# Order edges around the matrix-memory heads: query halves behind the score weighting, mask load first, conditioning row behind the target rows

## The chip, the cores and the metric

The kernel runs on one core of a Trainium2 chip. The metric is the device time of one execution, in microseconds (us); before the change it is 1218.85 us, the median of three runs (1218.58 to 1222.32). One core has five engines with a queue each, and each queue is worked off in order: TensorE (PE in the profile) multiplies matrices into eight accumulation banks, VectorE (DVE) and ScalarE (ACT) work element by element, GpSimd (POOL) does the same more slowly and here mostly issues transfers, and SyncE (SP) issues the other transfers.

## The reference, cut to what matters

One layer of a diffusion backbone works on 512 latent tokens and 256 context tokens of width 1024. The part that the change touches is the matrix-memory branch, which has four heads of 256 channels. For every head and each of two directions it computes decay-weighted scores and applies them to the values:

```python
s = jnp.einsum("bhtd,bhsd->bhts", qb, kb) * jnp.exp(logD - m_t[..., None])
num = jnp.einsum("bhts,bhsd->bhtd", s, vb) + ...
den = jnp.sum(s, axis=-1) + ...
hb = num / jnp.maximum(jnp.abs(den), jnp.exp(-m_t))[..., None]
```

The reference scans in chunks of 64 tokens. The kernel uses the equal form without the scan: for a target token t and a source token s, latent or context, the score q·k is multiplied by the exponential of (a row that depends on the target) + (a column that depends on the source), with a mask inside the diagonal block.

A second part is the conditioning: the vector c goes through silu and a matrix of 6 x 1024 columns, and the results shift, scale and gate the stream (`modT` in the kernel).

## The kernel before, in words

Every product keeps fp32 accuracy with three passes: each operand x is split into a high half (ScalarE copies it to a rounded 32-bit format, line 214) and a low half (VectorE subtracts the high half from x, line 215), and TensorE computes high·high, high·low and low·high into the same bank (lines 233 to 235). Nearly all TensorE time goes into these three lines, and a weight or an operand can be used only when both halves are there.

Loads that are to be split go through a ring of four staging buffers named `wr` (line 239 for weights, line 903 for the heads' operands; the conditioning weights `in_wada` use it too, line 357). A buffer of the ring is free when VectorE has made the low half, or has done the multiplication for the conditioning.

The kernel is written in program order, and a planner then sets the order of each engine's queue from estimated times; it may place later work ahead of earlier work if its estimate says that it is ready sooner. It also adds all waits. Two means are used to steer it: `behind()` (line 578) and `tc.issue_after(x)`. What is traced inside such a block, and runs on the engine of instruction x, is queued behind x on that engine. This fixes the order of issue; it is no wait for x to finish, and it has no effect on instructions of other engines.

The stage around the change (about 556 to 710 us) works like this:

- `load_head(h)` (line 910) loads queries (`wr<-qd`) and two key tiles (`wr<-kd`) of a head and splits them into `uh`/`ul` and the two `K` buffers. Queries have two buffers, so the next head's can be loaded while one is in use. Keys have one buffer for each half.
- `load_values(h)` (line 922) loads and splits the values into `vh`/`vl`, one buffer each.
- `target_rows()` (line 848) is done once: TensorE transposes 14 small tiles, and ScalarE copies them in four pieces into `rrow` (line 855).
- `decay(h, d)` (line 872) broadcasts a row with a matmul against the selector `sel` (line 880), adds the mask with another (line 882), and ScalarE takes exponentials of the banks into `dx` and `dy` (line 886).
- `weigh(h, ...)` (line 931) computes q·k for six source tiles s. Each takes six matmuls of 512 columns into a bank of the pool `psH`, which has four banks. VectorE multiplies the bank by 1/64 and by the decay tile (line 943), once for each direction; then the bank is free.
- `halves` (line 945) splits the weighted scores, and `values(h, d, ...)` (line 951) multiplies them with the values into the four banks of `psG` and divides by the denominator (lines 962 to 968).

The loop over heads (line 1354) does, for h = 0, 1, 2: `load_head(h+1)`, first `decay` of head h+1, `values(h, 0)`, second `decay`, one tile of the other branch's projection (`ph_tiles`, line 1299, for h = 1 and 2), `weigh(h+1)`, `values(h, 1)`, `load_values(h+1)`, `halves`, another projection tile, and `head_norm`. `ph_tiles` first reloads its 16 operand tiles from memory (`hTh<-hhd`, `hTl<-hhd`, lines 226 and 227), issued by GpSimd. Output gates are computed as fillers before that (`gate_tile`, line 702): ScalarE applies a tanh (line 708) and GpSimd stores the result (line 709).

`ada_row()` (line 378) makes the conditioning row `crow`: one load (line 380), one tanh on ScalarE (line 381) and two multiplications on VectorE (lines 382 and 383). `steps` and `beside` then advance the conditioning products (line 372).

Of the kernel before, what the change touches and what calls it, by code (L numbers as in the profile page):

```python
# [8 lines left out]
F32 = mybir.dt.float32  # L9
F32R = mybir.dt.float32r  # L10
AF = mybir.ActivationFunctionType
ALU = mybir.AluOpType
# [147 lines left out]
def build(nc, tc, I, out, dbg=None):  # L160
# [14 lines left out]
    act, dve, pe, gp = nc.scalar, nc.vector, nc.tensor, nc.gpsimd  # L175
    dma = nc.sync.dma_start
# [8 lines left out]
    def T(p, shape, dt=F32, tag=None, bufs=None):  # L185
        uid[0] += 1
        p = HOME.get(tag, p)
        bufs = BUFS.get(tag, bufs)
        kw = {} if bufs is None else {"bufs": bufs}
        nm = f"{tag or 't'}_{uid[0]}"  # L190
        return p.tile(list(shape), dt, tag=tag or nm, name=nm, **kw)
# [9 lines left out]
    def bank(p=None):  # L201
        return T(p or psH, [128, 512], F32, "bank")
# [5 lines left out]
    def load(p, key, shape, tag=None, src=None):  # L208
        t = T(p, shape, F32, tag or key)
        dma(t[:], I[key] if src is None else src)  # L210
        return t
# [51 lines left out]
    for key, shp in VECS:  # L263
        m = int(np.prod(shp))
# [113 lines left out]
    def ada_row():  # L378
        th = T(PW, [128, WMAX], F32, "wr")[:, :D]
        dma(crow[:], I["crow"].broadcast_to([128, D]))  # L380
        act.activation(th, crow[:], AF.Tanh, scale=0.5)
        dve.tensor_scalar_mul(crow[:], crow[:], 0.5)
        dve.scalar_tensor_tensor(crow[:], th, 1.0, crow[:], op0=ALU.add, op1=ALU.mult)
# [329 lines left out]
    def gate_math(p):  # L713
# [38 lines left out]
        ps = bank()  # L752
        L = ps[:, 0:48].rearrange("p (b d h) -> p b d h", b=6, d=2)
        fc = S([2, 6, 4], "fc")
# [93 lines left out]
    def target_rows():  # L848
        rr = T(PM_, [128, 512], F32R, "rrow")
        gp.memset(rr[:].bitcast(F32), 0.0)  # L850
        for q, (g0, n) in enumerate(((0, 4), (4, 4), (8, 3), (11, 3))):
            pr = bank()
            for j in range(n):
                pe.transpose(pr[:16, 128 * j : 128 * j + 128], G["rhl"][:, g0 + j].bitcast(F32), ident)
            act.activation(rr[32 * q : 32 * q + 16, : 128 * n], pr[:16, : 128 * n], AF.Copy)
        G["rr"] = rr

# [43 lines left out]
    def staged(src, n, hi, lo, a=None):  # L903
        t = T(PW, [128, WMAX], F32, "wr")[:, :n]
        if a:
            t = t.rearrange("p (a b) -> p a b", a=a)
        dma(t, src)
        split(hi, lo, t)

    def load_head(h):  # L910

        kh, kl = (T(PT, [128, 2048], F32R, "K")[:, :1536].rearrange("p (a b) -> p a b", a=2) for _ in range(2))
        qh, ql = T(PT, [128, 2, SEQ], F32R, "uh"), T(PT, [128, 2, SEQ], F32R, "ul")

        staged(qd[:, 2 * h : 2 * h + 2], 2 * SEQ, qh[:], ql[:], 2)
        if h == 0:
            fill(next(cf))
        for i in range(2):
            staged(kd[:, 2 * h + i], SEQ + CTX, kh[:, i], kl[:, i])
        return (qh, ql), (kh, kl)  # L920

    def load_values(h):
        Vh, Vl = T(PM_, [128, 6, NV], F32R, "vh"), T(PM_, [128, 6, NV], F32R, "vl")
        gp.memset(Vh[:, :, 256:257].bitcast(F32), 1.0)
        gp.memset(Vh[:, :, 257:258].bitcast(F32), 0.0)
        gp.memset(Vl[:, :, 256:258].bitcast(F32), 0.0)
        for b, n in ((0, 4), (4, 2)):
            staged(vd[:, h, b : b + n], 256 * n, Vh[:, b : b + n, :256], Vl[:, b : b + n, :256], n)
        return Vh, Vl

    def weigh(h, qq, kk, Dm):

        (qh, ql), (kh, kl) = qq, kk
        for s in (4, 5, 0, 1, 2, 3):
            ps = bank()
            tk = slice(128 * s, 128 * s + 128)
            for i in range(2):
                mm3(ps[:], kh[:, i, tk], kl[:, i, tk], qh[:, i], ql[:, i], i == 0, i == 1)
            for d in range(2):
                t0, n = PIECE[d][s][:2]  # L940
                dst = piece(Dm[d], d, s)
                sv = ps[:, 128 * t0 : 128 * (t0 + n)].rearrange("p (a b) -> p a b", a=n)
                dve.scalar_tensor_tensor(dst, sv, 1.0 / 64, dst, op0=ALU.mult, op1=ALU.mult)

    def halves(Dm):
        wh, wl = parts(F32R), parts(F32R)
# [3 lines left out]

    def values(h, d, W, V, den, hs):
        (wh, wl), (Vh, Vl) = W, V
        for t in range(4):
# [255 lines left out]
    def fill(n):  # L1209
        for _ in range(n):  # L1210
            if fills:
                fills.pop(0)()
# [68 lines left out]
    PM_ = PMS.enter_context(pool("pm", reuse_waits="tile"))  # L1281
# [29 lines left out]
    fill(next(cf))  # L1311
    L = load_head(0)
    fill(next(cf))
    V = load_values(0)
    sel = T(PM_, [128, 32], F32R, "sel")
    selr = load(PM_, "sel", [128, 32], "selr")
    act.activation(sel[:], selr[:], AF.Copy)
    mask = T(PM_, [128, 2, 128], F32R, "mask")
    maskr = load(PM_, "mask", [128, 2, 128], "s2")
    act.activation(mask[:], maskr[:], AF.Copy)  # L1320
    identr = T(PM_, [128, 128], F32R, "identr")
    act.activation(identr[:], ident, AF.Copy)
    target_rows()

    def steps(n):
        for _ in range(n):
            background()

    Dm = [decay(0, d) for d in range(2)]
    fill(next(cf))  # L1330
    ada_row()
    weigh(0, L[0], L[1], Dm)
    steps(2)
    fill(next(cf))
# [19 lines left out]
    for h in range(NH):  # L1354
        last = h == NH - 1
        den = T(PM_, [128, 2, 4], F32, "den", 2)
        hs = T(PM_, [128, 4, 256], F32, "hs", 2)
        if last:
            sp_ = [T(PT, [128, 2048], F32R, "K") for _ in range(2)]
            parts_ = [[v[:, 512 * j : 512 * j + 512] for j in range(4)] for v in sp_]  # L1360
            for i, tag in enumerate(("uh", "ul")):
                v = T(PT, [128, 2, SEQ], F32R, tag)
                parts_[i] += [v[:, 0], v[:, 1]]
            its = [iter(v) for v in parts_]
            hm = reload(hmd, lambda: next(its[0]), lambda: next(its[1]), range(4))
        else:
            L = load_head(h + 1)
            with behind():
                D0 = decay(h + 1, 0)
        values(h, 0, W[0], V, den, hs)  # L1370
        if not last:
            with behind():
                Dm = D0, decay(h + 1, 1)
            if h == 0:
                fill(len(fills))
            beside(h, 0)
            late()
            weigh(h + 1, L[0], L[1], Dm)
        values(h, 1, W[1], V, den, hs)
        if last:  # L1380
            late(True)
        else:
            V = load_values(h + 1)
            W = [halves(Dm[d]) for d in range(2)]
            beside(h, 1)
        with tc.high_priority(PR[0] if last else 0):
            head_norm(hs)
        done.append((h, hs, head_gate(h)))
# [189 lines left out]
    for d in range(KT):  # L1578
        ws = []
        for k0 in (0, 8, 16):  # L1580
            n = min(8, FT - k0)
# [28 lines left out]
```

## Time and profile before

| | |
|---|---|
| median of three runs | 1218.85 us |
| profiled execution: its time | 1219.83 us |
| profiled execution: its span, first to last instruction | 1218.0 us |
| TensorE busy with matmuls | 1180.8 us (97%) |
| VectorE busy | 833.2 us (68%) |
| ScalarE busy | 528.9 us (43%) |
| mean granted TensorE clock | 0.992 of full speed |
| moved by DMA | 189 MB, 155 GB/s on average |

A profile row of the timeline reads: start, duration, engine, line of the kernel, operation, output<-inputs, and in square brackets the idle time of the engine before it with what ended that. An L with a number is a line of the kernel. "SPq" and "POOL ... DMA" rows are the issue of a transfer; when it lands is told in the table of DMA issues. Buffer numbers are left out, so that `wr` is any of the ring's four buffers and `s` any of six scratch tiles (`s2` in the code). The rows by stretch of time give the length, the busy time and the number of instructions of PE, of weight loads on PE, of DVE, ACT and POOL, then the granted TensorE clock, the mean busy share of the DMA engines, and GB/s.

### The profile page before, as it was taken

How to read it: one execution, taken by the hardware profiler on the slowest of the kernel's cores; microseconds unless marked ns; L12 is line 12 of the kernel's file. 1: busy time of each engine (PE TensorE's matmuls, PEld its weight loads, DVE VectorE, ACT ScalarE, POOL GpSimd, SP SyncE). 2: the span in 40 equal slices, each digit the busy share in tenths (PEclk: the TensorE clock that was granted, in tenths of full speed). 3: DMA queues.
4: the chain of work that ended last, by engine and by line, in shares of the span. 5: the costliest groups of instructions: out<-in, count | busy, mean ns of one | idle time of the engine just before them, and what ended most of it. 6: DMA issues, size and time to landing. Idle time of an engine off the chain costs nothing.

```text
span 1218.0 us, 16831 instructions
## 1 busy us (share of the span) xinstructions
PE 1180.8 (97%) x6440; PEld 1012.9 (83%) x6440; DVE 833.2 (68%) x1336; ACT 528.9 (43%) x824; POOL 87.7 (7%) x168
## 2 busy tenths in 40 slices
PE   4999999999999999999989999999999999999997
PEld 2799988888888888888778988889888888888886
DVE  5967797978989999897758896767753434432332
ACT  3754465753545444453655642333432232322221
POOL 0011110100010010101032031000000000000000
PEclk9999999999999999999989999999999999999998
DMA  9744453364244353434695686773443333233312
GB/s 346 248 159 163 136 185 106 133 237 143 75 162 137 130 174 102 147 106 155 211 319 180 196 265 218 260 234 121 140 138 104 90 100 101 85 95 96 96 48 70
DMA packets 63377, 189.04 MB, mean 155 GB/s; under 512 B 8760, under 2 KB 12608, under 8 KB 61120
## 3 DMA queue, kind: packets, MB, share of 16 engines
q1 hardware_dynamic: 51536, 150.20, 38.6%
q0 software_dynamic: 11760, 37.76, 8.7%
q8 instruction: 51, 0.84, 0.3%
q14 instruction: 30, 0.25, 0.1%
HBM read 154.37 MB, written 33.55 MB: 154 GB/s over the span
## 4 chain that ended last, share of the span: by engine, by line
PE 89%; DVE 4%; DMA 3%; ACT 2%; issue 1%; POOL 0%; SPq 0%; DVEq 0%; POOLq 0%; ACTq 0%
PE bank L233 26%; PE bank L234 26%; PE bank L235 26%; PE bank L659 2%; PE bank L660 2%; PE bank L661 2%; DMA wr<-qd 1%; DMA wr<-in_wph 1%; PE bank L616 1%; PE bank L463 1%; DVE wl L215 1%; PE bank L464 1%; ACT wh L214 1%; DMA ul<-in_xT 1%; PE bank L337 0%
## 5 line engine op out<-in xcount | busy, mean ns | idle before, releaser
L233 PE MATMUL bank<-hTh,wh 128*128 128x512 f32 (+1 forms) x952 | 366.6, 387 | 2.9 <-ACT hTh L1094 2.0
L234 PE MATMUL bank<-hTl,wh 128*128 128x512 f32 (+1 forms) x952 | 366.1, 386 | 2.9 <-DVE hTl L1100 2.2
L235 PE MATMUL bank<-hTh,wl 128*128 128x512 f32 (+1 forms) x952 | 365.6, 385 | 0.0
L214 ACT ACTIVATE wh<-wr 128x1024 fp32r<-128x1024 f32 (+1 forms) x167 | 172.2, 1033 | 400.8 <-PE bank L234 205.1
L215 DVE TENSOR_TENSOR wl<-wr,wh 128x1024 fp32r<-128x1024 f32 (+1 forms) x167 | 197.8, 1187 | 170.9 <-ACT wh L214 169.6
L233 PEld LDWEIGHTS bank<-hTh,wh 128*128 128x128 f32 x952 | 178.9, 188 | 37.5 <-ACT hTh L1094 2.2
L234 PEld LDWEIGHTS bank<-hTl,wh 128*128 128x128 f32 x952 | 179.0, 188 | 36.8 <-DVE hTl L1100 2.5
L235 PEld LDWEIGHTS bank<-hTh,wl 128*128 128x128 f32 x952 | 179.0, 188 | 34.6
L233 PE MATMUL bank<-big,wh 128*128 128x512 f32 (+1 forms) x266 | 94.7, 356 | 0.0
L234 PE MATMUL bank<-big,wh 128*128 128x512 f32 (+1 forms) x266 | 94.6, 356 | 0.0
L235 PE MATMUL bank<-big,wl 128*128 128x512 f32 (+1 forms) x266 | 94.6, 355 | 0.0
L372 DVE SCALAR_TENSOR_TENSOR wr<-wr,crow 128x1024 f32<-128x1024 f32 x32 | 38.9, 1218 | 28.3 <-DMA wr<-in_wada 28.2
L233 PEld LDWEIGHTS bank<-big,wh 128*128 128x128 f32 x266 | 50.3, 189 | 7.2
L235 PEld LDWEIGHTS bank<-big,wl 128*128 128x128 f32 x266 | 50.3, 189 | 7.1
L234 PEld LDWEIGHTS bank<-big,wh 128*128 128x128 f32 x266 | 50.3, 189 | 7.1
L214 ACT ACTIVATE hb<-hb 128x512 fp32r<-128x512 f32 (+1 forms) x49 | 36.5, 767 | 33.3 <-DVE hb L468 18.5
L1554 DVE TENSOR_TENSOR s<-s,bank 128x512 f32<-128x512 f32 x22 | 15.1, 686 | 46.4 <-PE bank L235 46.4
L391 POOL TENSOR_TENSOR rr<-rv,negh 128x2 f32<-128x2 f32 (+1 forms) x6 | 5.5, 924 | 510.7 <-DVE rv L389 510.7
L215 DVE TENSOR_TENSOR hb<-hb,hb 128x512 fp32r<-128x512 f32 (+1 forms) x49 | 40.4, 858 | 2.0 <-ACT hb L214 1.8
L659 PE MATMUL bank<-wh,hTh 128*128 128x256 f32 (+1 forms) x128 | 36.4, 285 | 0.0
L661 PE MATMUL bank<-wh,hTl 128*128 128x256 f32 (+1 forms) x128 | 36.4, 285 | 0.0
L660 PE MATMUL bank<-wl,hTh 128*128 128x256 f32 (+1 forms) x128 | 36.4, 284 | 0.0
(383 smaller groups left out, 2208.2 us busy)
## 6 DMA issues: line engine op xcount, KB each, us to landing
wr<-in_win SPq DMA_DIRECT2D x64, 512.0 KB, 3.8
wr<-in_w SPq DMA_DIRECT2D x60, 512.0 KB, 3.5
wr<-in_wada SPq DMA_DIRECT2D x32, 512.0 KB, 4.1
Kd<-K POOLq DMA_DIRECT2D x8, 1024.0 KB, 4.7
K<-Kd SPq DMA_DIRECT2D x8, 1024.0 KB, 6.4
wr<-in_wv SPq DMA_DIRECT2D x8, 512.0 KB
gmd<-s POOLq DMA_DIRECT2D x16, 256.0 KB, 2.5
wr<-in_wph SPq DMA_DIRECT2D x8, 512.0 KB, 4.2
```

Of the source, the lines that this page charges most:

```text
L214: act.activation(hi, x, AF.Copy)
L215: dve.tensor_sub(lo, x, hi.bitcast(F32))
L233: pe.matmul(o, wh, xh, start=first, stop=False)
L234: pe.matmul(o, wh, xl, start=False, stop=False)
L235: return pe.matmul(o, wl, xh, start=False, stop=last)
L372: dve.scalar_tensor_tensor(w, w, 1.0, crow[:], op0=ALU.mult, op1=ALU.mult, accum_out=s)
L463: pe.matmul(ps[:], lhs, w4h, start=True, stop=False)
L464: pe.matmul(ps[:], lhs, w4l, start=False, stop=True)
L659: pe.matmul(o, xh, wh, start=bool(k == 0), stop=False)
L660: pe.matmul(o, xh, wl, start=False, stop=False)
L661: m = pe.matmul(o, xl, wh, start=False, stop=bool(k == KT - 1))
L1554: dve.tensor_tensor(t[:], t[:], pb[:], op=ALU.mult)
```

## The change

There are three parts.

1. `weigh` now records its last VectorE instruction, and in the loop over heads `load_head(h+1)` is traced behind it: the VectorE subtractions that make the low halves of the next head's queries and keys are queued behind the last multiplication of `weigh(h)`. Transfers and ScalarE copies of `load_head` are on other engines, and are under no new order.
2. The load of the mask is traced ahead of the load of the selector, and the selector's load, as well as the load inside `ada_row`, are queued behind it on SyncE.
3. `target_rows` returns its last ScalarE copy, and the tanh of `ada_row` is queued behind it on ScalarE.

```diff
@@ target_rows
-            act.activation(rr[32 * q : 32 * q + 16, : 128 * n], pr[:16, : 128 * n], AF.Copy)
+            m = act.activation(rr[32 * q : 32 * q + 16, : 128 * n], pr[:16, : 128 * n], AF.Copy)
         G["rr"] = rr
+        return m.ins
...
+    weighed = []
+
     def weigh(h, qq, kk, Dm):
...
-                dve.scalar_tensor_tensor(dst, sv, 1.0 / 64, dst, op0=ALU.mult, op1=ALU.mult)
+                m = dve.scalar_tensor_tensor(dst, sv, 1.0 / 64, dst, op0=ALU.mult, op1=ALU.mult)
+        weighed.append(m.ins)
...
+    maskr = T(PM_, [128, 2, 128], F32, "s2")
+    loaded = dma(maskr[:], I["mask"]).ins
     sel = T(PM_, [128, 32], F32R, "sel")
-    selr = load(PM_, "sel", [128, 32], "selr")
+    with tc.issue_after(loaded):
+        selr = load(PM_, "sel", [128, 32], "selr")
     act.activation(sel[:], selr[:], AF.Copy)
     mask = T(PM_, [128, 2, 128], F32R, "mask")
-    maskr = load(PM_, "mask", [128, 2, 128], "s2")
     act.activation(mask[:], maskr[:], AF.Copy)
...
-    target_rows()
+    rows = target_rows()
...
-    ada_row()
+    with tc.issue_after(loaded), tc.issue_after(rows):
+        ada_row()
     weigh(0, L[0], L[1], Dm)
...
         else:
-            L = load_head(h + 1)
+            with tc.issue_after(weighed[-1]):
+                L = load_head(h + 1)
```

## The prediction

> **What bounds the kernel now.** I read the totals first, then the waits of TensorE with what ended them, then the timeline around each of the two waits that the change can reach, and last the granted clock there.
>
> ```profile
> span 1218.0 us, 16831 instructions
> PE 1180.8 (97%) x6440; PEld 1012.9 (83%) x6440; DVE 833.2 (68%) x1336; ACT 528.9 (43%) x824; POOL 87.7 (7%) x168
> ```
> ```profile
> PE bank L233 <- DVE dx L943: 3.8, 2, 3.4
> ...
> PE bank L880 <- ACT rrow L855: 1.6, 1, 1.6
> ```
> TensorE is the bound; only its idle time, or a lower clock, can be won. Of its waits (in total, times, longest), those for line 943 and line 855 are the ones that the parts of the change touch, 5.4 us together. TensorE's timeline has them at these places:
>
> ```profile
> 582.16 1.04 PE L880 MATMUL bank<-rrow,sel 128*128 128x512 f32 x4 [1.58 <-ACT rrow L855]
> ...
> 621.45 0.39 PE L233 MATMUL bank<-uh,K 128*128 128x512 f32 x1
> ...
> 630.40 0.76 PE L233 MATMUL bank<-uh,K 128*128 128x512 f32 x1 [3.35 <-DVE dx L943]
> ...
> 642.50 0.39 PE L233 MATMUL bank<-hTh,wh 128*128 128x512 f32 x1
> ...
> 684.18 0.28 PE L233 MATMUL bank<-vh,dx 128*128 128x258 f32 x1
> ...
> 704.63 0.47 PE L233 MATMUL bank<-uh,K 128*128 128x512 f32 x1 [0.40 <-DVE dx L943]
> ```
> The stall of 3.35 us has a second price, in the stretches behind it (the clock is the third figure from the right):
>
> ```profile
> 582.00:583.00 1.00, 0.84 (x4) 0.79 (x5) 1.00 (x3) 0.54 (x3) 0.00 (x0) 1.00 0.96 172
> ```
> ```profile
> 630.00:631.00 1.00, 0.59 (x2) 0.53 (x3) 1.00 (x3) 0.11 (x1) 1.00 (x3) 0.50 1.12 354
> ...
> 635.00:636.00 1.00, 1.00 (x5) 0.81 (x4) 0.10 (x1) 0.53 (x1) 0.00 (x0) 0.50 1.25 391
> 636.00:637.00 1.00, 1.00 (x9) 1.00 (x8) 1.00 (x3) 1.00 (x2) 0.00 (x0) 0.85 1.25 381
> ```
> After 1.58 us idle the clock is still 1.00; after 3.35 us it is 0.50 until 636 and 0.85 for one more. From 630.40 to 636 half of 5.6 us is lost, 2.8 us, and then 0.15 us: **2.95 us** in all.
>
> **Part one, the query halves (line 215 behind line 943).** The queues of VectorE, ScalarE and SyncE tell how the stall came about.
>
> ```profile
> 620.66 0.17 DVE L1454 TENSOR_SCALAR g1h<-modT 128x8 f32<-128x8 f32 x1
> 627.84 1.22 DVE L215 TENSOR_TENSOR ul<-wr,uh 128x1024 fp32r<-128x1024 f32 x1 [7.00 <-ACT uh L214]
> 628.98 2.48 DVE L943 SCALAR_TENSOR_TENSOR dx<-bank,dx 128x512 f32<-128x512 f32 x4
> ```
> ```profile
> 626.75 1.06 ACT L214 ACTIVATE uh<-wr 128x1024 fp32r<-128x1024 f32 x1 [5.09 <-DMA wr<-qd]
> ```
> ```profile
> 619.24 0.33 SPq L907 DMA_DIRECT2D wr<-qd  x1
> ...
> 629.09 0.32 SPq L907 DMA_DIRECT2D wr<-kd  x1
> ```
> Head 2's queries leave at 619.24 and land 7.5 us later; their low half stands in VectorE's queue ahead of the weighting of head 1, so VectorE idles 7.00 us while TensorE, which began those scores at 621.45, fills four banks and stops. With the order turned, the first bank (six matmuls, 1.4 us) is weighted from 622.9 on, and one bank's two multiplications (a quarter of the 2.48 us row times two, 1.24 us) keep up with TensorE's 1.4 us. So the wait goes: **-3.35 us** (bounds -3.35 and 0, the zero being the second rival), and with it the clock loss: **-2.95 us** (same bounds).
>
> The page "TensorE: Matmul & The Clock Gate" of the Trainium skill (Part 1) puts the drop to half rate at one idle window of about 3.4 us, free-running. The trace agrees with its 3.35 us; by that rule a new stall below about 3 us would cost its length alone, which leaves the sum as it is, and a longer one would cost the clock again.
>
> What becomes late instead: the subtraction (1.22 us) moves behind the weighting, and with it the ring buffer that it frees. The second key load left at 629.09, as the subtraction ended; it now leaves behind the weighting, and SyncE's queue behind it waits along (a gate load, the next projection weights, the next conditioning weights, the values). At head 2 this is no later than before: the weighting, begun at 621.45 less 1.2 us and not stalled, ends on VectorE near 629, and the subtraction at 630.2.
>
> **What TensorE then runs into: the projection at 642.50.** It would come 7.5 us earlier (1.2 + 3.35 + 2.95), at 635.0, and it needs 16 tiles that GpSimd loads:
>
> ```profile
> 628.67 0.55 POOL L709 DMA_DIRECT2D gmd<-s  x1 [7.45 <-DMA wr<-kd]
> ...
> 633.07 0.53 POOL L227 DMA_DIRECT2D hTl<-hhd  x1
> ```
> ```profile
> hTl<-hhd POOLq DMA_DIRECT2D x1, 256.0 KB, 7.3
> ```
> The last one (the DMA row is that of the stretch 632.9 to 633.5) lands at 640.4. Eight steps of three matmuls at 0.23 us bring its use to 635.0 + 7 x 0.69 + 0.23 = 640.1, so 0.3 us are lost at once. The DMA engines are full there (391 GB/s in the row of 635): the key load beside them adds up to 384 KB, 1.0 us, and the next projection weights, which leave earlier, 512 KB, 1.3 us. Bounds 0 (GpSimd's queue is freed sooner) and **+2.6**; I take +0.9 us, the 0.3 with half of the key load.
>
> **The same edge at head 3** (weighting of head 2) removes no wait of TensorE, and it costs.
>
> ```profile
> 657.68 4.88 SPq L907 DMA_DIRECT2D wr<-kd  x2
> ```
> ```profile
> 660.99 1.23 DVE L215 TENSOR_TENSOR ul<-wr,uh 128x1024 fp32r<-128x1024 f32 x1 [3.26 <-ACT uh L214]
> ...
> 671.33 0.89 DVE L943 SCALAR_TENSOR_TENSOR dy<-bank,dy 128x128 f32<-128x128 f32 x2 [0.32 <-PE bank L235]
> ...
> 675.74 0.95 DVE L215 TENSOR_TENSOR K<-wr,K 128x768 fp32r<-128x768 f32 x1
> ...
> 680.64 1.21 DVE L215 TENSOR_TENSOR vl<-wr,vh 128x1024 fp32r<-128x1024 f32 x1
> ...
> 682.16 0.68 DVE L215 TENSOR_TENSOR vl<-wr,vh 128x512 fp32r<-128x512 f32 x1
> ```
> Before, the 1.23 us lay behind 3.26 us of idle time. Now they go in at 672.2, where VectorE has no idle time until the value halves are done at 682.84, and TensorE takes these at 684.18: 1.34 us of room, nearly used up. The chain that ended last goes through VectorE and the projection weights from there to the wait at 704.63, with no room at all:
>
> ```profile
> 682.87 4.56 DMA wr<-in_wph
> ...
> 703.88 0.61 DVE dx L943
> ```
> So **+1.2 us**; bound 0 from below, if small gaps take it. From above: the second key load now leaves at 673.4 in place of 662.2; landing takes
>
> ```profile
> wr<-kd SPq DMA_DIRECT2D x7, 384.0 KB, 3.6
> ```
> 3.6 us, the ScalarE copy 0.8 (three quarters of the 1.06 us of 1024 columns), so its low half can't begin before 677.8, 2.1 us past 675.74; if VectorE waits there in order, the cost is 3.3. At head 1 nothing changes: its subtraction already stood behind the weighting.
>
> **Parts two and three, mask, selector and conditioning row.**
>
> ```profile
> 578.29 1.06 ACT L381 ACTIVATE wr<-crow 128x1024 f32<-128x1024 f32 x1 [3.98 <-DMA crow<-in_crow]
> ...
> 579.83 2.19 ACT L855 ACTIVATE rrow<-bank 16x512 fp32r<-16x512 f32 x4
> 582.04 0.42 ACT L1320 ACTIVATE mask<-s 128x256 fp32r<-128x256 f32 x1
> ```
> ```profile
> 556.29 0.42 SPq L210 DMA_DIRECT2D selr<-in_sel  x1
> 573.34 0.33 SPq L380 DMA_DIRECT2D crow<-in_crow  x1
> ...
> 574.26 0.39 SPq L210 DMA_DIRECT2D s<-in_mask  x1
> ```
> ```profile
> s<-in_mask SPq DMA_DIRECT2D x1, 128.0 KB, 7.0
> ```
> ScalarE idled 3.98 us for the conditioning row's load before the tanh, with the copies into `rrow` behind it. Ahead of the tanh, they start when the transposes are there (near 578) and end near 580.2, before TensorE asks at 580.58; the whole 1.58 us could go. But the mask (issued at 574.26, landed 7.0 us later) must then be early too: if it leaves at 556, as the selector does now, all is well; if its scratch tile comes free only near 573, the selector, now queued behind it, leaves at 573.7, lands by the mask's time at 580.7, and the copies behind its cast end 1.1 us later than before. Bounds -1.6 and +1.1; I take **-1.2 us**, nearer to the first, since the queue of SyncE is empty from 556.7 to 573. The tanh, its two multiplications and the ring buffer of the tanh come some 2 us later; I cost that at nothing, because no wait of TensorE is on a weight's low half and four banks of 1.4 us lie between TensorE and VectorE in the first weighting; with that cover gone it is those 2 us.
>
> **The sum.** -1.2 - 3.35 - 2.95 + 0.9 + 1.2 = -5.4 us. The profiled execution took 1219.83 us (span 1218.0 and 1.83 around it), so 1214.4 in its terms; it lies 0.98 us above the median of 1218.85, against which the result is **1213.5 us**.
>
> **The rivals.** *Given back by late loads (0.20).* The wall at 640.4 costs 2.6 and head 3 costs 3.3: -7.5 + 5.9 = -1.6, 1217.3 us. For it: full DMA engines and full VectorE at the places named; against it: a wait at the one shortens the other's.
>
> *It doesn't do what it says (0.06).* The planner orders everything anew and puts other work that waits for a transfer, a weight's low half or a conditioning product, ahead of line 943. Then only -1.2 is left, 1217.7 us. Against it: from 620.66 to 627.84 VectorE's queue held nothing else.
>
> *A new long stall (0.12), slower.* The mechanism is one: the second key load, late by the new order, holds ScalarE and VectorE in order ahead of the values. It decides once that load takes about as long as the slowest in this stage:
>
> ```profile
> DMA to landing us min/median/max: 3.7/7.2/10.7
> ```
> (the `hTl` reloads). At 10.7 us it lands at 684.1, then 0.8, 0.95, 1.21 and 0.68 us bring the values to 687.7: 3.6 us past 684.18, long enough to halve the clock again, 6.55 us with it. The same at both heads gives 13.1 - 7.5 = +5.6, 1224.5 us; at one alone it falls among the given-back.
>
> **How the numbers follow.** A measurement of this kernel tells 0.3%, 3.7 us, from no change. The forecast has 0.62, and stands for faster (under 1215.2 us). Same takes the first two rivals, 0.26; slower is the third, 0.12. The forecast's own range runs from all bounds on the good side (-1.6 - 3.35 - 2.95) with the wait of 0.40 us at 704.63 gone too (-8.3, 1210.5 us) to 1215.2. The range that holds 8 in 10 takes in the first two rivals: 1210.5 to 1219.5 us, with most of the slower case left out above.
>
> **What would show it.** Right: no wait of TensorE on line 943 near 628, a clock of 1.00 throughout 625 to 640, `ul` of head 2 behind line 943, the four `rrow` copies ahead of the tanh, the mask issued near 556. The give-back: short waits of TensorE on `hTl` or `hTh` near 640 and on line 215 (`vl`) or 943 between 680 and 705. Wrong: VectorE idle in front of line 943 for a transfer, ScalarE idle on the selector near 580, or a wait above 3 us with a clock of 0.50 behind it in a new place.

## The result, and the profile after

The change makes the kernel slower. After: 1226.67 us, median of 11 runs (1223.27 to 1229.18); before, on the same chip: 1218.95 us, median of 11 (1217.98 to 1222.32). The ratio is 1.0056, with a 95% interval of 1.0044 to 1.0068; 1213.5 us had been forecast. The profiled execution took 1229.18 us, 9.35 us more than the one of before; it is the slowest of the 11, so what its trace adds up to is 1.6 us more than the 7.7 us between the medians. One profiled execution, that of the control with less to move, ran at a granted clock of 0.85 and took 1311.82 us; nothing is read from its trace.

The totals of the changed kernel show the same work in a longer span:

```profile
span 1227.1 us, 16829 instructions
PE 1183.7 (96%) x6440; PEld 1014.2 (83%) x6440; DVE 832.9 (68%) x1336; ACT 529.5 (43%) x824; POOL 87.4 (7%) x168
```
In TensorE's timeline the wait for the weighting near 628 and the one for line 855 are gone, and six others above 0.9 us are there; the rows without a wait are starts of stages (line 881 was 880 before, 946 was 943, 996 was 992):

```profile
581.28 0.47 PE L881 MATMUL bank<-rrow,sel 128*128 128x512 f32 x1 [0.37 <-issue]
...
598.07 0.50 PE L235 MATMUL bank<-hTh,wl 128*128 128x512 f32 x1 [1.66 <-DVE wl L215]
...
605.24 0.50 PE L233 MATMUL bank<-hTh,wh 128*128 128x512 f32 x1 [1.89 <-ACT wh L214]
...
621.35 0.44 PE L881 MATMUL bank<-rrow,sel 128*128 128x384 f32 x1 [0.95 <-ACT dy L887]
...
626.63 0.39 PE L233 MATMUL bank<-uh,K 128*128 128x512 f32 x1
...
634.79 0.28 PE L233 MATMUL bank<-vh,dx 128*128 128x258 f32 x1
...
652.06 0.51 PE L234 MATMUL bank<-vl,dx 128*128 128x258 f32 x1 [3.32 <-DVE vl L215]
...
666.61 0.60 PE L996 MATMUL bank<-mats,hs 128*128 128x128 f32 x4
...
701.77 0.60 PE L996 MATMUL bank<-mats,hs 128*128 128x128 f32 x4
...
706.57 0.50 PE L233 MATMUL bank<-uh,K 128*128 128x512 f32 x1 [1.01 <-ACT s L999]
...
713.11 0.47 PE L233 MATMUL bank<-uh,K 128*128 128x512 f32 x1 [2.44 <-DVE dx L946]
...
722.91 0.40 PE L233 MATMUL bank<-hTh,wh 128*128 128x512 f32 x1
```
The rows of the kernel before that answer to four of these:

```profile
635.66 0.42 PE L233 MATMUL bank<-vh,dx 128*128 128x258 f32 x1
...
662.05 0.60 PE L992 MATMUL bank<-mats,hs 128*128 128x128 f32 x4
...
697.22 0.60 PE L992 MATMUL bank<-mats,hs 128*128 128x128 f32 x4
...
714.06 0.39 PE L233 MATMUL bank<-hTh,wh 128*128 128x512 f32 x1
```
Stage by stage, both executions laid side by side:

| from | to | before | after | difference |
|---|---|---|---|---|
| start | target row transposes (line 854) | 577.04 | 577.60 | +0.56 |
| transposes | first score of head 1 (621.45; 626.63) | 44.41 | 49.03 | **+4.62** |
| first score of head 1 | first value of head 0, second direction (635.66; 634.79) | 14.21 | 8.16 | **-6.05** |
| that | transposes of head 0's output (662.05; 666.61) | 26.39 | 31.82 | **+5.43** |
| that | transposes of head 1's output (697.22; 701.77) | 35.17 | 35.16 | 0 |
| that | projection behind head 3's scores (714.06; 722.91) | 16.84 | 21.14 | **+4.30** |

The sum is +8.85 of the 9.35. So the forecast gain at the weighting was there, and three losses outweigh it. The granted clock (third figure from the right) of the changed kernel adds to two of them:

```profile
652.00:653.00 1.00, 0.94 (x4) 0.94 (x5) 1.00 (x5) 0.00 (x0) 0.10 (x1) 0.58 0.97 303
653.00:654.00 1.00, 1.00 (x7) 1.00 (x6) 0.86 (x2) 0.00 (x0) 0.98 (x2) 0.50 0.63 164
654.00:655.00 1.00, 1.00 (x7) 1.00 (x7) 0.67 (x4) 0.88 (x3) 0.29 (x1) 0.50 0.82 270
655.00:656.00 1.00, 1.00 (x8) 1.00 (x8) 0.75 (x6) 0.78 (x3) 0.56 (x1) 0.71 1.10 340
```
That is 0.42 + 0.5 + 0.5 + 0.29 = 1.71 us lost; from 713 to 718 the figures are 0.80, 0.50, 0.50, 0.50 and 0.99, 1.71 us again.

What stands behind the waits is seen on ScalarE, VectorE and SyncE of the changed kernel, in this order:

```profile
589.03 1.21 ACT L381 ACTIVATE wr<-crow 128x1024 f32<-128x1024 f32 x1
...
592.76 1.05 ACT L214 ACTIVATE wh<-wr 128x1024 fp32r<-128x1024 f32 x1
...
631.98 1.06 ACT L214 ACTIVATE uh<-wr 128x1024 fp32r<-128x1024 f32 x1 [4.46 <-DMA wr<-qd]
632.95 1.04 ACT L214 ACTIVATE dx<-dx 128x1024 fp32r<-128x1024 f32 x1
...
644.53 0.85 ACT L214 ACTIVATE K<-wr 128x768 fp32r<-128x768 f32 x1 [2.99 <-DMA wr<-kd]
645.28 0.21 ACT L966 ACTIVATE den<-bank 128x1 f32<-128x1 f32 x2
645.38 1.58 ACT L214 ACTIVATE vh<-wr 128x1024 fp32r<-128x1024 f32 x2
```
```profile
593.41 3.47 DVE L946 SCALAR_TENSOR_TENSOR dy<-bank,dy 128x512 f32<-128x512 f32 x8
596.80 1.22 DVE L215 TENSOR_TENSOR wl<-wr,wh 128x1024 fp32r<-128x1024 f32 x1
...
634.02 1.23 DVE L215 TENSOR_TENSOR dx<-dx,dx 128x1024 fp32r<-128x1024 f32 x1 [2.22 <-ACT dx L214]
...
637.56 1.21 DVE L215 TENSOR_TENSOR ul<-wr,uh 128x1024 fp32r<-128x1024 f32 x1
...
692.97 0.95 DVE L215 TENSOR_TENSOR K<-wr,K 128x768 fp32r<-128x768 f32 x1
```
```profile
592.95 5.41 SPq L362 DMA_DIRECT2D wr<-in_wada  x2
599.19 0.33 SPq L254 DMA_DIRECT2D wr<-in_win  x1
...
638.83 0.32 SPq L908 DMA_DIRECT2D wr<-kd  x1
...
680.54 0.32 SPq L908 DMA_DIRECT2D wr<-kd  x1
...
693.94 0.33 SPq L254 DMA_DIRECT2D wr<-in_wph  x1
```
**The conditioning row.** The tanh of line 381 ran at 578.29 before; now it runs at 589.03, behind the exponentials of both decays of head 0. Its own ring buffer is free only when the second multiplication of the row ends at 592.90, and the conditioning products behind it hold theirs, so the next conditioning weights leave at 592.95 (before 581.40) and the next projection weights at 599.19 (before 583.81); a weight's low half stands behind the weighting of head 0, until 598.02. These are the waits at 598.07 and 605.24.

**Head 2.** The second key leaves at 638.83 (before 629.09), as the query's subtraction (from 637.56) frees its buffer. ScalarE comes to its copy at 641.54, idles 2.99 us, and the row sums and the value halves stand behind it in the queue. TensorE waits 3.32 us for the low value halves and loses the 1.71 us of the clock: 0.40 + 3.32 + 1.71 = 5.43 us, with a short wait at the projection (0.40), the whole of that row.

**Head 3.** The second key leaves at 680.54 (before 662.24), and VectorE makes its low half only at 692.97 (before 675.74). That frees its buffer at 693.92, and the projection weights leave at 693.94 (before 682.87). Their copies and subtractions fall among the weighting of head 3: 1.01 + 2.44 + 1.71 - 0.60 (the two waits there before) = 4.56, for 4.30 in the table.

### The profile page after: what moved, and what is told of

Same layout as the page of the kernel before. It is cut to its first block, busy times and chain, and to the rows that moved or that the text cites. A ratio compares the mean times of both kernels' runs of the same rounds, so it can differ in the third digit from the quotient of the medians.

```text
span 1227.1 us, 16829 instructions
## 1 busy us (share of the span) xinstructions
PE 1183.7 (96%) x6440; PEld 1014.2 (83%) x6440; DVE 832.9 (68%) x1336; ACT 529.5 (43%) x824; POOL 87.4 (7%) x168
## 4 chain that ended last, share of the span: by engine, by line
PE 89%; DVE 4%; DMA 3%; ACT 2%; issue 1%; POOL 0%; SPq 0%; DVEq 0%; POOLq 0%
PE bank L233 26%; PE bank L234 26%; PE bank L235 26%; PE bank L659 2%; PE bank L660 2%; PE bank L661 2%; DMA wr<-in_wph 1%; PE bank L616 1%; PE bank L463 1%; PE bank L464 1%; ACT wh L214 1%; DVE wl L215 1%; DMA wr<-qd 1%; DMA ul<-in_xT 1%; DMA wr<-kd 0%
```

## The experiments

All were timed beside the kernel before, whose medians were 1218.98 to 1219.17 us. First the parts alone.

**Part one, all heads** (the query halves behind the weighting; nothing of mask and row):

```diff
-            L = load_head(h + 1)
+            with tc.issue_after(weighed[-1]):
+                L = load_head(h + 1)
```


> Part one alone: the low halves of load_head behind the last multiplication of weigh, for all heads; mask, selector and conditioning row as before. Theory A (each part has its own price, read from the trace of after: the edge gains 6.0 us at the weighting of head 1, and loses 5.4 us at head 2's values and 4.3 us at the weighting of head 3, since the second key load waits for a ring buffer): 1222.6 us, no wait on line 943 near 628, and a wait of TensorE of 2 to 3.5 us on the value halves (vl) near 650. Theory B (the edge is sound, and the late conditioning row of the other parts holds the ring and makes everything behind it late): about 1213.5 us, no wait on vl near 650.

Measured: 1222.48 us, ratio 1.0029 (1.0019 to 1.0038). The stall at the weighting is gone; in its place are waits of 1.4 us on the row sums, 2.8 us on the low value halves of head 1 and 2.0 us on the weighting of head 3, the last two each followed by a clock loss. The edge, without the other parts, already costs more than it wins.

**Part one, head 2 only** (the same edge with the condition `h == 1`):

> Part one for head 2's loads alone, the only place where TensorE waited for it (load_head(2) behind weigh(1)); heads 1 and 3, mask and conditioning row as before. Theory A: -6.0 us for the stall and its clock, +5.4 us for the values at head 2, nothing at head 3: -0.6 us, 1218.3 us, with a wait on vl of 2 to 3.5 us. Theory B: -6 us with up to 1 us given back, 1213 to 1214 us.

Measured: 1219.30 us, ratio 1.0005 (0.9996 to 1.0015). The 6 us won at the weighting come back within 20 us, as 1.34 us on the row sums and 3.2 us on the value halves, with the clock loss behind. (The profiled execution, 1221.85 us, is 2.5 us above the median; half rate lasted 6.8 us in it.) The edge at the other heads costs 1222.48 - 1219.30 = 3.2 us.

**Mask part alone** (mask first, selector and conditioning row's load behind it):

```diff
+    maskr = T(PM_, [128, 2, 128], F32, "s2")
+    loaded = dma(maskr[:], I["mask"]).ins
...
-    selr = load(PM_, "sel", [128, 32], "selr")
+    with tc.issue_after(loaded):
+        selr = load(PM_, "sel", [128, 32], "selr")
...
-    ada_row()
+    with tc.issue_after(loaded):
+        ada_row()
```


> Part two alone: mask loaded first, selector and conditioning row's load behind it on SyncE; the tanh has no edge, the heads are as before. Theory A: the tanh of the conditioning row goes behind the exponentials of both decays, its ring buffer is held some 10 us longer, TensorE waits 1.7 us on wl and 1.9 us on wh near 600, and the stall at the weighting of head 1 stays in some form: +4.6 us, 1223.5 us. Theory B: the whole loss lies here and the stall at the weighting of head 1 comes on top: 1227 us or more.

Measured: 1226.42 us (median of six), ratio 1.0058 (1.0042 to 1.0073), between the two theories. The largest loss of all the parts. Its profiled execution, 1223.40 us, is the fastest of the six, so 3 us of the loss are in no trace. The edge that puts the tanh behind `rrow` isn't in this kernel, yet the tanh runs at 587.99, behind all exponentials of both decays: with the mask early, the planned order has the decays ahead. TensorE waits 1.66 us for a weight's low half and 1.72 us for a high half near 600. So the mask load, not the row edge, moved the tanh.

**Row part alone** (`ada_row()` behind the `rrow` copies, mask as before):

```diff
-    ada_row()
+    with tc.issue_after(rows):
+        ada_row()
```


> Part three alone: the tanh of the conditioning row behind the four copies into rrow on ScalarE; mask, selector and heads as before. Both theories: the tanh stands right behind the copies, since without the early mask nothing draws the exponentials ahead of it. Theory A: the 1.58 us wait on rrow shrinks to what the late mask leaves of it, -1.5 to 0 us, 1217.4 to 1219 us. Theory B (a late conditioning row is what holds the ring): the row is 2 to 4 us later, so a part of the loss shows: +1 to +3 us.

Measured: 1220.55 us, ratio 1.0017 (1.0008 to 1.0026). The tanh runs at 580.78, right behind the mask's cast, and the wait for `rrow` falls from 1.58 to 0.54 us; a wait of 1.7 us turns up at the projection near 642. A gain of 1 us in one place was given back in another, and the time lies in the band of the theory of the late row.

**Mask and row, with the tanh held ahead of the exponentials:**

```diff
-    Dm = [decay(0, d) for d in range(2)]
     fill(next(cf))
-    ada_row()
+    with tc.issue_after(loaded), tc.issue_after(rows):
+        conditioned = ada_row()
+    with tc.issue_after(conditioned):
+        Dm = [decay(0, d) for d in range(2)]
```


> Parts two and three without part one, and the tanh of the conditioning row kept early: the gate filler and the conditioning row are traced ahead of the first decays, whose exponentials are queued behind the tanh on ScalarE. Theory A (in the mask-only run it was the late tanh, holding a ring buffer, that cost): no wait of TensorE on wl or wh near 600, the wait on rrow gone, the stall at the weighting of head 1 as before: -1.5 to 0 us against before, 1217.4 to 1219 us. Theory C (the early mask itself, by the other order of the exponentials and matmuls, cost): 1223 us or more, as with the mask alone.

Measured: 1220.71 us, ratio 1.0016 (1.0006 to 1.0025). By the medians most of the loss of the mask part goes (1226.42 to 1220.71), and with it the two waits on weight halves near 600, so the tanh's late place made these. It isn't all: in place of one wait of 1.58 us there are five of 0.18 to 0.77 us between 586 and 591, 2.2 us together, with a clock loss behind them. From the transposes to the first score of head 1 this trace takes 47.59 us, the mask part alone 48.85, the kernel before 44.41; so in this stage this kernel loses even with the tanh early.

**Queries off the ring.** If the ring buffer were all, loading the next queries straight into `ul` and subtracting there in place should free it; once without and once with the edge of part one:

```diff
-        staged(qd[:, 2 * h : 2 * h + 2], 2 * SEQ, qh[:], ql[:], 2)
+        raw = ql[:].bitcast(F32)
+        dma(raw, qd[:, 2 * h : 2 * h + 2])
+        act.activation(qh[:], raw, AF.Copy)
+        dve.tensor_sub(ql[:], raw, qh[:].bitcast(F32))
```
(for heads 1 to 3)

> The query load off the ring alone, with no edge of order. Theory A: the load leaves when its own buffer is free, well ahead of the weighting, so its low half no longer stops VectorE: no wait on line 943 above 1 us near 628, 1212.5 to 1215 us, and the edge of part one is not needed. Theory D: the loads of this stage fill the DMA engines all the same, the low half lands late ahead of line 943 and the stall stays: 1218 us or more.

> Part one for all heads, with the query load of heads 1 to 3 taken off the ring: it goes straight into the buffer of the low half, and the subtraction is done in place. Theory A (the edge costs because the second key load and the loads behind it wait for the ring buffer of the queries): no wait on vl near 650, none above 1 us near 709, -6.0 us for the stall with up to 2 us given back, 1213 to 1215 us. Theory D (the edge costs because VectorE is full behind the weighting): the wait on vl stays above 2 us, 1218 us or more.

Measured: 1218.81 us without the edge, ratio 0.9992 (0.9983 to 1.0001); 1221.39 us with it, 1.0019 (1.0010 to 1.0027). In both the stall at the weighting is gone, and in both TensorE then waits at the next projection (4.21 and 2.70 us); with the edge it also waits 2.86 us at the weighting of head 3. Neither theory has the time right. ScalarE, VectorE and TensorE of the kernel without the edge:

```profile
636.33 1.06 ACT L920 ACTIVATE uh<-ul 128x1024 fp32r<-128x1024 f32 x1 [5.32 <-DMA ul<-qd]
```
```profile
637.41 1.23 DVE L921 TENSOR_TENSOR ul<-ul,uh 128x1024 fp32r<-128x1024 f32 x1 [4.66 <-ACT uh L920]
638.56 0.48 DVE L974 SCALAR_TENSOR_TENSOR hs<-bank,den,hs 128x256 f32<-128x256 f32 x1
```
```profile
639.14 0.62 PE L233 MATMUL bank<-hTh,wh 128*128 128x512 f32 x1 [4.21 <-ACT dy L214]
```
The load into `ul` leaves only at 628.21, when the scores of head 1 are done (SyncE waits 5.1 us for the last of their matmuls; why it does, with two buffers for the queries, isn't shown), so the queries come late. ScalarE idles 5.32 us in front of their copy and VectorE 4.66 us in front of their subtraction. Behind that stands VectorE's reading of a bank, until 639.04, and TensorE's projection starts at 639.14. The wait has changed its place, not its cause.

**Both mendings together** (queries off the ring, tanh held ahead):

> The query load off the ring together with mask first and the conditioning row kept early behind the rrow copies. Theory A: the two gains add, 1211 to 1214 us. Theory C or D: one of them or both are missing, 1217 us or more.

Measured: 1221.54 us, ratio 1.0017 (1.0007 to 1.0026), so the gains don't add; again ScalarE idles for the queries (3.92 us) and TensorE waits at the projection (2.81 us).

These pointed to one cause: a copy that waits for a late load, with work in ScalarE's queue behind it. **The second key behind the value halves** tests it; the edge is there for head 2 alone:

```diff
         for i in range(2):
-            staged(kd[:, 2 * h + i], SEQ + CTX, kh[:, i], kl[:, i])
+            with ExitStack() as es:
+                for m in valued if h == 2 and i else ():
+                    es.enter_context(tc.issue_after(m))
+                staged(kd[:, 2 * h + i], SEQ + CTX, kh[:, i], kl[:, i])
```
(`valued` holds the last load, copy and subtraction of `load_values`)

> The head-2 edge alone (query half of head 2 behind the weighting of head 1, nothing else of the change), and in addition the second key of head 2 is copied behind the value halves of head 1 on ScalarE and VectorE. Its load still leaves behind the query's half, as before. Theory A (order): the 6 us won at the weighting are lost because ScalarE idles 2.9 us in front of the second key, with the row sums and the value halves behind it in order. With the key behind them the waits of 1.34 us on the row sums and of 3.2 us on the value halves go, and the clock loss behind them: 1212 to 1215 us. Theory B (transfers): the DMA engines are full from 620 to 640 us and the reloaded projection rows, issued late because GpSimd's queue waits on ScalarE, bring a wait of 2 us or more at the projection: 1217 us or more.

Measured: **1216.09 us** (1215.35 to 1218.42), ratio 0.9977 (0.9968 to 0.9986): faster than before by 0.23%, the only kernel of the study that does the whole work and has its interval clear of 1 on this side. Against the same edge without this, 3.2 us. The time is 1 us above the band of the theory of order and below that of the theory of transfers. ScalarE of this kernel:

```profile
636.29 0.21 ACT L969 ACTIVATE den<-bank 128x1 f32<-128x1 f32 x2
...
636.74 1.57 ACT L214 ACTIVATE vh<-wr 128x1024 fp32r<-128x1024 f32 x2
640.64 1.06 ACT L214 ACTIVATE wh<-wr 128x1024 fp32r<-128x1024 f32 x1 [2.32 <-DMA wr<-in_wph]
641.60 0.83 ACT L214 ACTIVATE K<-wr 128x768 fp32r<-128x768 f32 x1
```
Row sums and value halves no longer stand behind the key, which finds its load landed when its turn comes. The stretches of the same kernel show TensorE nearly without idle time and the clock whole, with the DMA engines as full up to 640 as with the edge alone (1.07 in both):

```profile
620.00:640.00 20.00, 19.85 (x113) 17.45 (x112) 15.97 (x35) 11.09 (x19) 6.58 (x15) 1.00 1.07 351
640.00:660.00 20.00, 20.00 (x119) 17.82 (x119) 15.03 (x38) 13.75 (x32) 4.00 (x5) 1.00 0.57 178
```
So full DMA engines (the rival of this run) don't by themselves hold TensorE up in this stage. In the trace the 6.05 us won at the weighting of head 1 stay won up to the transposes of head 0's output; 1.6 us go later, at heads 2 and 3 (36.05 us for 35.17 and 17.60 for 16.84 in the last two rows of the table).

**All of head 2's copies behind the value halves**, without the edge (`weights` holds the last load of weights, so its loads are queued behind that one too):

```diff
-            L = load_head(h + 1)
+            with ExitStack() as es:
+                for m in valued + weights if h == 1 else ():
+                    es.enter_context(tc.issue_after(m))
+                L = load_head(h + 1)
```


> In place of the edge of the change, all copies of head 2's queries and keys stand behind the value halves of head 1, on ScalarE as on VectorE; mask, selector and conditioning row are as before. Theory A (order): ScalarE no longer waits for queries ahead of the gate, the decay halves and the row sums, so neither the stall at the weighting (3.35 us) nor one at the projection or the values of head 1 is left, and the clock stays 1.00 from 620 to 660: 1211 to 1214 us. Theory B (transfers): the projection behind the values of head 0 waits 2 us or more for its rows, with a clock loss behind it: 1217 us or more.

Measured: 1218.40 us, ratio 0.9992 (0.9983 to 1.0000). The first half of the expectation holds: no stall at the weighting or the projection, clock 1.00 from 560 to 660. The time doesn't follow, because the queries and the first key now keep their ring buffers until behind the values, and the second key leaves only at 640.44, when the values free one; ScalarE idles 3.39 us for it, and the scores of heads 2 and 3 wait 1.2, 1.4 and 1.5 us.

**Less to move.** The low halves of the projection rows aren't reloaded (eight loads of 256 KB less; the high halves stand in for them, so the output isn't the reference's), without and with the head-2 edge:

> The kernel before with one load left out: the low halves of the projection rows of the stage from 615 to 641 us aren't reloaded (eight loads of 256 KB less), the high halves stand in for them, so the output isn't the reference's. A control for the next run. Theory A (order) and B (transfers) both: the queries land earlier, so the stall of 3.35 us at the weighting shrinks to between 0 and 2.5 us and the clock loss with it: 1212 to 1217 us.

> The same load left out (low halves of the projection rows, so the output isn't the reference's), with the head-2 edge alone on top. Theory B (transfers): with 2 MB less to move the gain of the edge shows, the waits of 1.34 and 3.2 us go, 1211 to 1213 us, and 2 us or more below the control. Theory A (order): the second key still leaves only behind the query's half, near 635 us, lands some 4 us later instead of 5.6, and ScalarE still waits in front of it with the values behind: a wait of 1 us or more on the value halves stays, and the time is within 1.5 us of the control or above it.

Measured: 1218.70 us, ratio 0.9996 (0.9987 to 1.0006), and 1217.59 us, 0.9984 (0.9975 to 0.9993). The control missed its expectation: 2 MB less bought nothing there. In the kernel with the edge the mean DMA share from 620 to 640 falls from 1.07 to 0.81, but not where the queries are in flight: 0.98 in place of 1.01, and they take 6.75 us from issue to copy in place of 7.29. While the second key is in flight it is 0.42 in place of 1.12; the key takes 3.30 us in place of 5.58, ScalarE idles 0.59 us for it in place of 2.87, and the wait on the value halves falls from 3.20 to 0.92 us. With the edge the time is 1.1 us below the control, as the theory of order had it, not the 2 us or more of the theory of transfers. But the two go together: how long ScalarE stands in front of the key depends on the key's transfer, and who waits behind it depends on the order.

**The whole change with the second key behind the values of head 1:**

> The whole change, with one thing more: the second key of head 2 is copied behind the value halves of head 1 on ScalarE and VectorE (on ScalarE its queue differs from that of the change by this one copy). Theory A (order: the change's loss at head 2 is that copy, in front of the row sums and the value halves): the wait of 3.3 us on the value halves and the clock loss behind it go, 4 to 6 us below the change, 1220.5 to 1222.7 us; what is left above before is the mask part and head 3. Theory C (the gain at the weighting comes back somewhere else in any case): within 1.5 us of the change, 1225 us or more.

Measured: 1222.11 us, ratio 1.0033 (1.0021 to 1.0044), 4.6 us below the change by the medians. On ScalarE, between 626 and 665 us, this kernel differs from the changed one by the place of a single copy. The wait on the value halves is gone, the clock from 640 to 660 is 1.00 (0.91 in the changed kernel).

**Part one at all heads, with the second keys moved.** The edit has `h >= 2`, not the `h == 2` of the runs before: the second key of head 3 too stands behind the value halves of head 2, which the expectation doesn't say.

> Part one of the change at all heads, without the mask and row parts, and the second key of head 2 behind the value halves. Against the kernel with the head-2 edge and the late key (1216.1 us) only the edge at heads 1 and 3 is added. Theory A (head 3 loses by a chain of its own: query half late, staging buffer late, second key and then the projection weights late in SyncE's queue): the same 3 us as between the head-2 edge alone and the edge at all heads, 1218.5 to 1220 us, with a wait of 1.5 us or more on the weighting of head 3. Theory D (head 3 lost only because the stage before it ended late): 1215.5 to 1217 us.

Measured: 1218.08 us, ratio 0.9992 (0.9980 to 1.0003), between the two theories. From the transposes of head 1's output to the projection it takes 18.52 us, against 17.60 with the edge and the late key at head 2 only and 16.84 before; the wait on the weighting of head 3 is 1.71 us, and no clock is lost behind it. The whole change with head 2's key alone moved, the run above, takes 18.77 us there, so the place of head 3's key matters little. So head 3 has a loss of its own, 0.9 to 1.9 us in these traces, and in the changed kernel, with 21.14 us, a clock loss of 1.71 us came on top.

**The key's place alone, without the edge:**

> Only the second key of head 2 behind the value halves, no edge: the query half stays ahead of the weighting. Theory A (each of the two places holds a queue up by itself): the stall of 3.35 us at the weighting and its clock loss stay, and nothing is won, 1217.5 to 1220 us. Theory E (the key's place alone is what the faster kernel gains by): 1215 to 1217 us.

Measured: 1220.98 us, ratio 1.0017 (1.0007 to 1.0027). The stall is there (3.57 us), as expected; the time is 1 us above the band. The edge and the key's place pay only together.

**Edge at head 2, late key, and the row part:**

> The head-2 edge with the late key (1216.1 us), and in addition the conditioning row's tanh behind the target rows' copies on ScalarE (selector and mask loads as before). If the wait of 1.6 us for the target rows is worth its length once the later stages hold: 1214.5 to 1215.5 us. If, as the row part alone showed (1.6 us above before), the later tanh costs more than it wins: 1216.5 to 1219 us.

Measured: 1217.78 us, ratio 0.9991 (0.9982 to 1.0000): 1.7 us above the kernel without the row part. The wait for `rrow` falls to 0.54 us; ScalarE idles 6.22 us for the queries, and the projection waits 2.16 us.

## Why the prediction was wrong, point by point

- **The stall and the clock at the weighting, -3.35 and -2.95: right.** The stage shrank by 6.05 us of the 6.30, and the clock is 1.00 through it, as the part on what would show it asked.
- **The wait for `rrow`, -1.2: right** (1.58 to 0.37 us), and the mask left early, at 561.01. From there the prediction said "all is well", and that was the trap.
- **The tanh "I cost at nothing": the first step that failed.** It was to come some 2 us later, with the cover that no wait of TensorE is on a weight's low half. It came 10.7 us later. The step took the planner's order as fixed and moved only the tanh in it; an early mask makes the decays ready early, and they went ahead of the tanh, which the mask part alone shows. The wait of 1.66 us is one on a weight's low half. The stage lost 4.62 us net: the waits grew from 1.58 to 4.87 us, and the other 1.3 us lie in the same 220 matmuls standing wider apart. Of these I can lay some to each restart (0.44 to 0.50 us in place of 0.39); the rest is open. The trace of the mask part alone loses 4.43 us in the same stage. By the medians the mask and row parts cost 4.2 us beside part one (1226.67 - 1222.48), and 4.0 with head 2's key moved (1222.11 - 1218.08, where the second kernel has head 3's key moved too).
- **The projection, +0.9: on the good side**, 0.40 us, but by luck: what ended that wait in the trace are the row sums on ScalarE (line 966), not the rows that GpSimd loads, which the sum had priced.
- **"At head 2 this is no later than before": the second step that failed**, and the one that turned the sign of part one. The estimate was that the subtraction would end at 630.2 and the key leave about then. In the changed kernel the key left 12.2 us after the first score, not 10.0 (620.25 to 630.2 in the estimate). Within the weighting VectorE makes the low half of a decay tile at 634.02, after 2.22 us idle for its high half, which stands on ScalarE (632.95) behind the queries' copy of 631.98: the edge turned VectorE's queue, not ScalarE's, and the queries still hold it up there. The chain key, ScalarE, values was in the prediction, as the rival "a new long stall" with 0.12, priced for a slow load of 10.7 us. It didn't need one: the key took 5.7 us from issue to copy. The rival's mechanism came true at head 2 through the late issue, with an ordinary landing; the wait above 3 us with a clock of 0.50 behind it, named as a sign of being wrong, is the one at 652.06. The run with the key behind the values shows it: the copy's place is worth 3.2 us there, 4.6 in the whole change.
- **Head 3, +1.2 (bound 3.3): mis-sized.** It measured +4.30 in the trace, +3.2 by the medians (heads 1 and 3 together). The subtraction's 1.2 us were counted and the key's place on VectorE; what was named but given no price is the projection weights behind the key: they wait for buffers that the key frees late, and four of them came late. Put at nothing was also the clock, 1.71 us behind the waits.
- **What was said of the clock rule.** The prediction let new stalls under about 3 us cost only their length, by the page "TensorE: Matmul & The Clock Gate" of the Trainium skill (Part 1). The trace disagrees: 2.44 us of idle time cost 1.71 us more. The kernel before already showed it. The clock of its stretch from 629 to 630 is 0.74, so half rate began near 629.5, when TensorE had been idle since 627.05, some 2.4 us, and still had 0.9 us to wait:

```profile
629.00:630.00 1.00, 0.00 (x0) 0.00 (x0) 1.00 (x3) 0.00 (x0) 1.00 (x3) 0.74 1.07 381
```

Added one after the other, the parts measure: the edge at head 2 +0.3 us, at the other heads +3.2, mask and row +4.2, together the 7.7 us by which the change is slower. The split depends on the order of adding: alone the mask part costs 7.4 us and the row part 1.6, and with part one's 3.5 that is 12.5, so the losses overlap.

## What to carry to other kernels

An order edge moves a wait; it removes it only if nothing that is needed stands behind the waiting instruction in its new queue. So before a late load's copy is moved, follow its staging buffer to the next load, that load's copy to its place in the in-order queue, and ask who stands behind it; here one key copy behind the values turned +0.05% into -0.23%. And where a planner orders the queues, an input made early is an edit to everything that it makes ready: look at the planned order of the whole stage, not only at the instruction that was meant.

## What the runs showed of the hardware

**A clock loss comes in steps of one size.** TensorE's row of the kernel with part one at all heads and the keys moved, at the wait for `rrow`, and two stretches of 3.41 us there:

```profile
582.73 1.09 PE L880 MATMUL bank<-rrow,sel 128*128 128x512 f32 x4 [1.83 <-ACT rrow L855]
```
```profile
580.16:583.57 3.41, 1.58 (x8) 1.05 (x7) 3.34 (x5) 2.87 (x7) 0.54 (x1) 1.00 0.94 330
583.57:586.99 3.42, 3.42 (x10) 2.68 (x9) 0.75 (x2) 3.29 (x9) 0.00 (x0) 0.50 0.77 284
```
The clock is half for the whole of the second stretch: 1.71 us lost. After the waits of 3.32 and 2.44 us in the changed kernel and of 4.21 us with the queries off the ring it is 1.71 us too. (The stall of 3.35 us in the kernel before cost more, 2.95 us; there half rate went on for 5.9 us after the restart.)

**Whether it comes isn't told by the wait's length.** After 1.83 us it came here; after 1.84 us (queries off the ring, with the edge), 2.16 us (edge at head 2, late key and row part) and 2.38 us (tanh held ahead, at the weighting) it didn't. The page "TensorE: Matmul & The Clock Gate" of the Trainium skill (Part 1) says that the window runs free and is 3.4 us long. The traces agree with the length: in each of them all changes of the clock lie on a grid of 3.41 us. They don't show that idle time of a whole window is needed. What tells in most cases is the idle time inside one window of that grid. Above, the window ahead of the drop holds the whole 1.83 us; the wait of 1.84 us lies across a border, with 0.78 us on one side and 1.06 us on the other:

```profile
578.78:582.19 3.41, 2.63 (x16) 1.84 (x13) 1.68 (x2) 2.76 (x5) 0.54 (x1) 1.00 0.98 374
582.19:585.61 3.42, 2.36 (x11) 1.95 (x11) 2.62 (x5) 2.93 (x9) 0.00 (x0) 1.00 0.87 297
```
The waits of 2.16 and 2.38 us lie across a border in the same way (1.25 and 0.91 us; 1.07 and 1.30 us). In all the traces read here, between 150 and 1190 us, 15 of 17 drops follow a window with 1.83 us or more of idle time, and no window with more than 1.76 us goes without one; half rate went on for a second window in the four cases where the first had 0.5 us or more idle, the kernel before among them. Two drops follow windows with only 1.24 and 1.39 us idle, among the short waits near 590 (tanh held ahead, alone and with the queries off the ring); why isn't shown. So a kernel may lose or keep 1.7 us at one wait, by where the borders fall. That this widens the spread of the changed kernel's runs is likely: the four of the 11 with a mean clock of 0.991 or 0.992 took 1226.89 to 1229.18 us, the seven with 0.994 or more 1223.27 to 1227.18.

**How long a load took followed the DMA share while it was in flight.** In the two kernels with the edge at head 2, with and without the 2 MB, the key took 5.58 us at a DMA share of 1.12 and 3.30 us at 0.42, the queries 7.29 us at 1.01 and 6.75 us at 0.98. Leaving loads out helped only the load that they had run beside; these are two pairs, and other causes weren't tested.
